# A first stage in written order with filter products ahead in several banks, and a recurrence whose first head has places of its own

## The chip, the cores and the metric

The kernel runs on one core of one Trainium2 chip. The metric is the time of one execution in device microseconds (us); lower is better. A core has a matrix engine (TensorE, PE), a vector engine (VectorE, DVE), a scalar engine for functions and copies (ScalarE, ACT), a general engine (GpSimd, POOL) and a queue that issues transfers (SyncE, SP). Each has its own in-order stream of instructions; they wait for each other by semaphores.

## The reference

Three blocks follow each other on one sequence of 512 positions with 1024 features. Only the first block and one part of the second matter here.

Block 1 norms x, scales and shifts it by a condition c, and gives the result h to three branches:

```
mod   = silu(c) @ w_ada + b_ada            # shift, scale, gate: 1024 values each
h     = rmsnorm(x) * norm_g * (1 + scale) + shift
a     = attention over 8 heads of 64 (q, k, v, z from h @ w_in; a table of relative positions as bias)
b     = gated linear recurrence over 8 heads of 128: f = lb + (1 - lb) * sigmoid(fb),
        state = f * state + (1 - f) * k v, output silu(qb) * state, gated by silu(zb)
x     = x + gate * ((sigmoid(ga) * (a @ w_a) + sigmoid(gb) * (b @ w_b)) @ w_out)
```

Block 2 holds a long convolution whose filter depends on the weights alone: a small network of three sine layers gives 512 filter values for each of 512 channels, times a decay; the convolution is done by its spectrum. It also holds an embedding p @ w_ple that is needed late. Neither depends on x, so the kernel computes both before everything else.

## The kernel before

Everything is kept transposed: eight tiles of 128 features by 512 positions. A matrix is multiplied in two parts, high and low, to keep fp32 accuracy: each weight (128 x 1024, a "raw" tile by DMA) is cast on ACT into `wh` (L110), and DVE or POOL subtracts to give `wl` (L111); each activation is split the same way (`split`, L202 and L204). `acc_T` (L128) then issues three matmuls for each 128 rows, so a projection (`proj_T`, L138) is 24 matmuls of 512 columns. There are four raw places, three places for split weights, and eight PSUM banks: three "mm", two "s", two "t", one "o".

A scheduler orders the instructions of each engine by its own simulated timeline, except inside `manual_schedule`, which keeps the written order for the engines named. Where a region's instructions fall among those written outside of it stays the scheduler's choice.

The first stage is `start` (L486). It loads and computes, side by side:

- the filter network: `layer` (L1198, three times: two small matmuls, seven DVE operations to reduce the angle, a sine on ACT), then `filt(t)` for four tiles of positions (two fp32 matmuls from 64 rows in the "s" banks, a product with the decay on DVE L1234, a sum and a difference L1241, and their splits), then `spectrum(f)` for two halves of the spectrum: per half 24 matmuls in the "mm" banks (function `halves`), copies by ACT (L1251, L1252), a sum and a difference on POOL, four stores issued by ACT (L1256);
- the embedding: `emb`, eight tiles of six matmuls, copied into tiles of A and stored;
- the condition's scale and shift: `AdaRows` (L453). Each loads eight rows of 128 x 1024 (tile `adar`, six places for both), and four matmuls of 32 x 256 for each row add up in the bank "o"; `columns` copies the sum out (`adarow`, L473) and turns it;
- the norm of x: squares on ACT (L513), added on DVE (L515), `col_sums`, `rsqrt` (a power on POOL, L251), `rows`;
- h: `x` is scaled on DVE (L525), then each of eight tiles gets its shift and is split into A (ACT L533, DVE L534);
- `rel_table`: a small table for the attention's bias, stored to memory.

Then `attn1` (L544) runs four pairs of heads. Before its last values it opens a region in which PE keeps the written order, which lasts through the recurrence `hgrn` (L755). `last_values` turns the softmax weights of the last pair by PE and multiplies them with v, four steps; between them it issues the 24 matmuls of the recurrence's first forget projection (`w1fb[0]`) as filler. `hgrn` opens a pool `hg` whose places overlap those of attention. `Head.f` makes tanh, Ln (L795, L796) and a scan over positions (L800) with `reset`; `gated` makes q and z (tanh on ACT, a DVE product); `between` and `operands` make for each of seven levels a difference of cumulated logarithms (POOL L841, L842), its exponential (ACT L843) and two products (DVE L846, L847); `products` multiplies them on PE.

## Time and profile before

| what | us |
|---|---|
| median of 3 runs (lowest, highest) | 2259.17 (2255.76, 2261.93) |
| the profiled execution's own time | 2263.86 |
| its span | 2262.1 |
| first projection of attention starts | 84.75 |
| first head's products on PE start | 256.79 |

The page shows one execution by the hardware profiler. Engine rows give busy time; rows of operations give the line, the engine, output<-inputs by tile names, shape and count; in square brackets stands the idle time before an operation and what released it. "PE" counts matmuls, "PEld" the loading of their weights. The clock is the share of full speed that TensorE was granted.

### The profile page before, as it was taken

How to read it: one execution, taken by the hardware profiler on the slowest of the kernel's cores; microseconds unless marked ns; L12 is line 12 of the kernel's file. 1: busy time of each engine (PE TensorE's matmuls, PEld its weight loads, DVE VectorE, ACT ScalarE, POOL GpSimd, SP SyncE). 2: the span in 40 equal slices, each digit the busy share in tenths (PEclk: the TensorE clock that was granted, in tenths of full speed). 3: DMA queues.
4: the chain of work that ended last, by engine and by line, in shares of the span. 5: the costliest groups of instructions: out<-in, count | busy, mean ns of one | idle time of the engine just before them, and what ended most of it. 6: DMA issues, size and time to landing. Idle time of an engine off the chain costs nothing.

```text
span 2262.1 us, 30194 instructions
## 1 busy us (share of the span) xinstructions
PE 2193.2 (97%) x11672; PEld 1793.4 (79%) x11672; DVE 1372.2 (61%) x2226; ACT 947.0 (42%) x1597; POOL 529.1 (23%) x454
## 2 busy tenths in 40 slices
PE   7898999999999998999999999999999999999998
PEld 4677788888888976688888886798888788888886
DVE  6564777753354598478647647877666754433333
ACT  4344556642243456544324434455544233222221
POOL 3233555521122225221001103000111221310220
PEclk7899999999999999999999999999999999999999
DMA  8552122224323342233232243222222422223322
GB/s 317 183 162 75 54 94 85 84 75 130 103 88 110 115 136 75 68 109 101 79 110 102 70 153 118 87 83 75 80 95 83 140 84 94 94 83 112 98 79 76
DMA packets 80728, 235.27 MB, mean 104 GB/s; under 512 B 9887, under 2 KB 10911, under 8 KB 80584
## 3 DMA queue, kind: packets, MB, share of 16 engines
q1 hardware_dynamic: 65768, 208.25, 28.2%
q10 hardware_dynamic: 14816, 25.08, 3.4%
q8 instruction: 92, 1.51, 0.3%
q14 instruction: 52, 0.43, 0.1%
HBM read 218.60 MB, written 15.22 MB: 103 GB/s over the span
## 4 chain that ended last, share of the span: by engine, by line
PE 56%; DVE 2%; issue 2%; ACT 1%; POOL 0%; POOLq 0%; DVEq 0%; ACTq 0%
PE mm L116 49%; PE s L116 3%; PE o L116 2%; PE t L116 1%; DVE sg L1772 0%; PE t L1612 0%; ACT wh L110 0%; DVE x L2438 0%; DVE st L1597 0%; DVE wl L111 0%; DVE x L1773 0%; DVE B L212 0%; PE t L2123 0%; ACT A L211 0%; PE t L2086 0%
## 5 line engine op out<-in xcount | busy, mean ns | idle before, releaser
L116 PE MATMUL mm<-A,wh 128*128 128x512 f32 x2176 | 691.1, 393 | 1.0 <-DVE A L212 1.0
L110 ACT CAST wh<-wr 128x1024 fp32r<-128x1024 f32 (+2 forms) x374 | 368.4, 987 | 609.6 <-PE mm L116 398.5
L111 DVE TENSOR_TENSOR wl<-wr,wh 128x1024 fp32r<-128x1024 f32 (+3 forms) x371 | 446.2, 1204 | 275.4 <-ACT wh L110 274.3
L116 PE MATMUL mm<-B,wh 128*128 128x512 f32 x1672 | 536.2, 396 | 1.3 <-DVE us L268 0.9
L116 PEld LDWEIGHTS mm<-A,wh 128*128 128x128 f32 x2176 | 409.6, 189 | 89.3 <-issue 1.9
L116 PE MATMUL mm<-A,wl 128*128 128x512 f32 x1088 | 425.8, 392 | 4.3 <-DVE wl L111 4.3
L116 PEld LDWEIGHTS mm<-B,wh 128*128 128x128 f32 x1672 | 313.5, 188 | 72.7 <-issue 4.0
L116 PE MATMUL mm<-B,wl 128*128 128x512 f32 x836 | 329.2, 394 | 0.0
L116 PEld LDWEIGHTS mm<-A,wl 128*128 128x128 f32 x1088 | 205.4, 189 | 47.7 <-DVE wl L111 6.3
L116 PEld LDWEIGHTS mm<-B,wl 128*128 128x128 f32 x836 | 157.3, 188 | 35.0 <-issue 3.0
L251 POOL TENSOR_TENSOR r<-r,mhalf 128x4 f32<-128x4 f32 (+1 forms) x40 | 53.2, 1332 | 407.6 <-DVE r L250 407.6
L116 PE MATMUL mm<-a,wh 128*128 128x512 f32 x448 | 140.5, 389 | 0.0
L268 DVE TENSOR_TENSOR us<-mm,bc 128x512 f32<-128x512 f32 x95 | 65.1, 688 | 97.2 <-PE mm L116 95.8
L204 POOL TENSOR_TENSOR a<-sl,a 128x512 fp32r<-128x512 f32 x28 | 40.5, 1446 | 274.2 <-ACT a L202 274.2
L116 PEld LDWEIGHTS mm<-a,wh 128*128 128x128 f32 x448 | 84.1, 188 | 17.5
L116 PE MATMUL mm<-a,wl 128*128 128x512 f32 x224 | 86.8, 389 | 0.0
L116 PE MATMUL mm<-wh,A 128*128 128x256 f32 x448 | 84.8, 285 | 0.0
L116 PEld LDWEIGHTS mm<-wh,A 128*128 128x128 f32 x448 | 71.0, 191 | 1.2 <-issue 0.6
L2358 POOL TENSOR_TENSOR sl<-sl,bc 128x512 f32<-128x512 f32 x22 | 28.7, 1305 | 167.6 <-DVE sl L1718 167.6
L116 PE MATMUL mm<-wl,A 128*128 128x256 f32 x224 | 63.6, 284 | 0.0
L116 PE MATMUL mm<-wh,B 128*128 128x256 f32 x320 | 61.2, 287 | 0.0
L1747 DVE TENSOR_TENSOR x<-x,mm 128x512 f32<-128x512 f32 x32 | 22.0, 687 | 64.5 <-PE mm L116 64.5
(588 smaller groups left out, 3472.0 us busy)
## 6 DMA issues: line engine op xcount, KB each, us to landing
wr<-w2upg SPq DMA_DIRECT2D x22, 512.0 KB, 3.4
wr<-w2upu SPq DMA_DIRECT2D x22, 512.0 KB, 3.4
wr<-w3fg SPq DMA_DIRECT2D x22, 512.0 KB, 3.4
wr<-w3fu SPq DMA_DIRECT2D x22, 512.0 KB, 3.4
adar<-w1ada SPq DMA_DIRECT2D x16, 512.0 KB, 7.6
wr<-w3out SPq DMA_DIRECT2D x16, 512.0 KB, 3.5
wr<-w1ib SPq DMA_DIRECT2D x14, 512.0 KB, 3.5
wr<-w2uh SPq DMA_DIRECT2D x12, 512.0 KB, 3.4
```

Of the source, the lines that this page charges most:

```text
L110: nc.scalar.copy(out=hi[:, :n], in_=r[:, :n])
L111: (eng or nc.vector).tensor_tensor(out=lo[:, :n], in0=r[:, :n], in1=hi[:, :n].bitcast(F32), op=ALU.subtract)
L116: return self.nc.tensor.matmul(out, a, b, start=start, stop=stop)
L204: eng.tensor_tensor(out=l[:p], in0=src, in1=hi[:p].bitcast(F32), op=ALU.subtract)
L251: nc.gpsimd.tensor_tensor(out=r, in0=r, in1=self.mhalf[:, :n], op=ALU.pow)
L268: self.nc.vector.tensor_tensor(out=out, in0=ps, in1=bc, op=ALU.mult)
L1747: k.nc.vector.tensor_tensor(out=xs[n], in0=xs[n], in1=ps, op=ALU.add)
L2358: nc.gpsimd.tensor_tensor(out=s, in0=s, in1=norm.bc, op=ALU.mult)
```

## The change

The first stage is written as one order for PE, ACT, DVE, POOL and SP. Modulation rows are stepped through two or four at a time instead of all at once; the scale rows have four places, the shift rows are loaded as halves into the tiles of A. Filter products are separated from their use (`filt_ps`, in "s" and "mm" banks by turns). All four sums and differences of the filters are on DVE, all their low parts on POOL. Embeddings and the copies of the spectrum get tiles `e0` to `e7` of their own; their stores are issued by SP, at the end of what they belong to. The first weight of attention (`w1q[0]`) is loaded and split inside the region and handed on in `k.first`.

In attention's end, the forget projection `w1fb[0]` is issued on PE ahead of `last_values`, whose filler is now `w1qb[0]`. The first head's `k`, `b` and `q` (h0), `lvl` and `reset` are in the outer pool, and the first tanh depends on the last exponential of the softmax. For the first head, the differences of levels 0 and 2 are on DVE. The four zero fills (`ADs`, `near`) come after the first operands.

The core of the diff:

```diff
 def proj_T(...)
-            self.acc_T(ps, self.w(s, nk * P, eng), act, nk, i == 0, i == len(nks) - 1, k0=k0)
+            w, self.first = self.first or self.w(s, nk * P, eng), None
+            self.acc_T(ps, w, act, nk, i == 0, i == len(nks) - 1, k0=k0)
...
 class AdaRows
-    def load(self):
+    def load(self, kks, places=None):
         k = self.k
-        for kk in range(NK):
-            self.r.append(self.pool.tile([P, D], F32, tag="adar", bufs=6, name=k.name("adar")))
-            k.nc.sync.dma_start(out=self.r[kk], in_=k.aps["w1ada"][self.part, kk])
+        for kk in kks:
+            src = k.aps["w1ada"][self.part, kk]
+            if places:
+                r = places[kk]
+                for j in range(2):
+                    k.nc.sync.dma_start(out=r[j], in_=src[:, j * T : (j + 1) * T])
+            else:
+                t = self.pool.tile([P, D], F32, tag="adar", bufs=4, name=k.name("adar"))
+                k.nc.sync.dma_start(out=t, in_=src)
+                r = (t[:, :T], t[:, T:])
+            self.r.append(r)
...
 def start(k, early):
-    with k.tc.tile_pool(name="b1s", bufs=1) as pool:
+    with k.tc.tile_pool(name="b1s", bufs=1) as pool, k.tc.manual_schedule(
+        engines={E.PE, E.Activation, E.DVE, E.Pool, E.SP}
+    ):
+        scale, shift = AdaRows(k, pool, 1), AdaRows(k, pool, 0)
         early.load0(pool)
+        rb, oh = rel_load(k, pool)
...
+        scale.load(range(4))
         early.load1()
...
+        places = [[t.bitcast(F32) for t in k.A(i)] for i in range(NK)]
+        shift.load(range(4), places)
...
+        early.layer(0)
+        early.parts(0)
+        early.sin()
+        early.parts(1)
+        early.emb(2)
+        early.layer(1)
+        early.emb(2)
+        early.sin()
+        early.layer(2)
+        square(2)
+        scale.step(2)
+        early.emb(2)
+        square(2)
+        early.sin()
+        scale.step(2)
+        scale.load(range(4, 8))
+        shift.load(range(4, 6), places)
+        early.load_fw(0)
+        shift.load(range(6, 8), places)
+        early.load_fw(1)
+        early.emb(2)
+        early.filt_ps(0)
+        square(4)
+        early.filt_ps(1)
+        sums = k.col_sums(acc)
+        early.filt(0)
+        r = k.rsqrt(sums, NT, 1.0 / D)
+        early.filt_ps(2)
+        shift.step(2)
+        bc = k.rows(r)
+        early.filt(1)
+        scale.step(4)
+        early.filt_ps(3)
+        early.store()
+        early.filt(2)
+        shift.step(2)
         sc1 = scale.columns()
+        early.fparts(0)
+        early.filt(3)
...
+        early.halves(0, 0)
+        shift.step(4)
         sh = shift.columns()
+        early.fparts(1)
+        tab = rel_table(k, rb, oh)
...
+            if i == 4:
+                early.halves(0, 1)
+
+        k.first = k.w(k.aps["w1q"][0])
+        early.halves(1, 0)
+        early.halves(1, 1)
+        early.sums()
...
 def last_values(pr, pts, v, z2):
-            w = k.w(k.aps["w1fb"][0])
+            w = k.w(k.aps["w1qb"][0])
...
                 ordered.enter_context(k.tc.manual_schedule(engines={mybir.EngineType.PE}))
+                ahead.append(k.proj_T([k.aps["w1fb"][0]], h))
                 ahead.append(last_values(pr, pts, cur[2], z2))
...
 class Head, f
+                tile = lambda tag, i: p.tile([P, T], F32, tag=tag, bufs=2, name=k.name(tag)) if hd else h0[i]
+                kk, b = self.kk, self.b = tile("k", 0), tile("b", 1)
+                t = nc.scalar.activation(out=kk, in_=ps, func=AF.Tanh, scale=0.5)
+                if hd == 0:
...
+                    k.tc.add_manual_dep(t.ins, k.last_exp.ins.name, info, reason="functions of the scalar engine")
...
 operands
+                    eng = nc.vector if self.hd == 0 and li in (0, 2) else nc.gpsimd
+                    eng.tensor_tensor(out=dv[:, :, 0], in0=mid, in1=bv[:, :, 0], op=ALU.subtract)
+                    eng.tensor_tensor(out=dv[:, :, 1], in0=bv[:, :, 1], in1=mid, op=ALU.subtract)
...
 hgrn, the loop over heads
             cur.operands(range(4))
+            if hd == 0:
+                for t in ADs + near:
+                    nc.gpsimd.memset(t, 0.0)
...
 block1
+        h0 = [op.tile([P, T], F32, tag=f"h0{i}", name=f"h0{i}") for i in range(3)]
+        lvl = op.tile([P, 256], F32, tag="lvl", name="lvl")
+        k.nc.scalar.dma_start(out=lvl, in_=k.aps["c_lvl"])
+        reset = op.tile([P, T], F32, tag="reset", name="reset")
+        k.nc.scalar.dma_start(out=reset, in_=k.aps["c_reset"])
...
 class Early2
+    def filt_ps(self, t):
+        k = self.k
+        r = slice(t // 2 * 64, t // 2 * 64 + 64)
+        self.fps[t] = []
+        for j in range(2):
+            ps = k.bank(*(("mm", 3) if t % 2 else ("s", 2)))
+            k.mm(ps, self.cur[r, t % 2 * P : t % 2 * P + P], self.wo[r, j * 512 : (j + 1) * 512], True, True)
+            self.fps[t].append(ps)
...
     def filt(self, t):
-            (nc.gpsimd if add else nc.vector).tensor_tensor(out=s, in0=fb[0], in1=fb[1], op=op)
-            l.append(k.split(k.pair(p, f"{nm}{t}"), s, lo="v" if add else "g"))
+            nc.vector.tensor_tensor(out=s, in0=fb[0], in1=fb[1], op=op)
+            l.append(k.split(k.pair(p, f"{nm}{t}"), s, lo="g"))
...
+    def fparts(self, f):
+        self.fw_parts.append(self.k.parts(self.cw[f], eng=None if f else self.k.nc.gpsimd))
...
+    def sums(self):
+        nc = self.k.nc
+        for f, j, (a, b) in self.ab:
+            d = self.tmp()
             nc.gpsimd.tensor_tensor(out=d, in0=a, in1=b, op=ALU.subtract)
-            nc.gpsimd.tensor_tensor(out=a, in0=a, in1=b, op=ALU.add)
+            nc.vector.tensor_tensor(out=a, in0=a, in1=b, op=ALU.add)
             for i, s in enumerate((a, d)):
-                nc.scalar.dma_start(out=self.kf[j, 2 * f + i], in_=s)
+                nc.sync.dma_start(out=self.kf[j, 2 * f + i], in_=s)
```

More of the change, by code (lines that the diff above doesn't have):

```diff
@@ L136, in acc_T @@
             self.mm(ps, wh, al[:, :n], False, stop and k == nk - 1)
+    first = None
     def proj_T(self, srcs, act, tag="mm", bufs=3, nks=(8,), eng=None):
@@ L495, in start @@
             xs.append(x)
+        scale.load(range(4))
         early.load1()
-        early.load_fw(0)
-        early.load_fw(1)
-        scale, shift = AdaRows(k, pool, 1), AdaRows(k, pool, 0)
-        scale.load()
+        places = [[t.bitcast(F32) for t in k.A(i)] for i in range(NK)]
+        shift.load(range(4), places)
         c = k.v("c", 0, 8)
@@ L537, in start @@
             h.append((hi, lo))
-        with k.tc.issue_after(mark):
-            early.spectrum(1)
-            tab = rel_table(k, pool)
+            if i == 4:
[4 more added lines that the diff above has]
+        early.sums()
     return h, tab
@@ L803, in qz @@
                 if i == 0:
-                    self.q = gated(self.hd, "w1qb", "q")
+                    first = {} if self.hd else {"ps": ps0[1], "o": h0[2]}
+                    self.q = gated(self.hd, "w1qb", "q", **first)
                 else:
@@ L961, in hgrn @@
         cur, old = Head(0), None
-        cur.f(f0)
+        cur.f(ps0[0])
         cur.qz(0)
@@ L1045, in block1 @@
             with ordered:
-                hgrn(k, h, *lb, ob, op, fill, v0, ahead[1])
+                hgrn(k, h, *lb, ob, op, fill, (v0, ahead[1:], h0, lvl, reset))
             return block1_end(k, h, oa, ob, gate, first, xp(), done)
@@ L1179, in load0, with parts @@
         self.fw = [self.load(nm, 64) for nm in ("fw1", "fw2", "fw3")]
-        self.cw, self.sm, self.df = [], [], []
-        pt = [p.tile([P, T], F32, tag=f"pt{i}", name=f"pt{i}") for i in range(2)]
+        self.cw, self.sm, self.df, self.we, self.pa, self.es = [], [], [], [], [], []
+        self.ws, self.fw_parts, self.ab = [], [], []
+        self.pt = [p.tile([P, T], F32, tag=f"pt{i}", name=f"pt{i}") for i in range(2)]
         for i in range(2):
-            nc.sync.dma_start(out=pt[i], in_=k.aps["pT"][:, i * T : (i + 1) * T])
-        self.we = [k.parts(k.raw(k.aps["w2ple"][i]), eng=None) for i in range(2)]
-        self.pa = [k.split(k.pair(p, f"pa{i}"), pt[i], lo="g") for i in range(2)]
+            nc.sync.dma_start(out=self.pt[i], in_=k.aps["pT"][:, i * T : (i + 1) * T])
+            self.ws.append(k.raw(k.aps["w2ple"][i]))
+    def parts(self, i):
+        k = self.k
+        for j in (0, 1) if i == 0 else ():
+            self.pa.append(k.split(k.pair(self.p, f"pa{j}"), self.pt[j], lo="g"))
+        self.we.append(k.parts(self.ws[i]))
     def load1(self):
@@ L1211, in layer, with sin, emb @@
         clamp_pi(k, h)
-        nc.scalar.activation(out=h, in_=h, func=AF.Sin)
         self.cur = h
-    def emb(self, ns):
+    def sin(self):
+        self.k.nc.scalar.activation(out=self.cur, in_=self.cur, func=AF.Sin)
+    def emb(self, m):
         k, p, nc = self.k, self.p, self.k.nc
-        for n in ns:
+        for n in range(len(self.es), len(self.es) + m):
             hi, lo = self.we[n // 4]
@@ L1221, in emb, with store @@
             k.acc_T(ps, (hi[:, o:], lo[:, o:]), self.pa, 2)
-            e = k.A(n)[0].bitcast(F32)
+            e = p.tile([P, T], F32, tag=f"e{n}", name=f"e{n}")
             nc.scalar.copy(out=e, in_=ps)
-            nc.sync.dma_start(out=self.ed[n], in_=e)
+            self.es.append(e)
+    def store(self):
+        for n, e in enumerate(self.es):
+            self.k.nc.sync.dma_start(out=self.ed[n], in_=e)
+    def filt_ps(self, t):
+        k = self.k
+        r = slice(t // 2 * 64, t // 2 * 64 + 64)
[4 more added lines that the diff above has]
+            self.fps[t].append(ps)
+    fps = {}
     def filt(self, t):
@@ L1228, in filt @@
         fb = []
-        for j in range(2):
-            ps = k.bank("s", 2)
-            r = slice(t // 2 * 64, t // 2 * 64 + 64)
-            k.mm(ps, self.cur[r, t % 2 * P : t % 2 * P + P], self.wo[r, j * 512 : (j + 1) * 512], True, True)
+        for ps in self.fps[t]:
             f = self.tmp()
```

90 lines of the change are left out of this document (43 added, 47 removed).

## The prediction

> **What bounds the kernel now.** I read the page first: is one engine the bound, and where is it not full?
>
> ```profile
> span 2262.1 us, 30194 instructions
> ...
> PE 2193.2 (97%) x11672; PEld 1793.4 (79%) x11672; DVE 1372.2 (61%) x2226; ACT 947.0 (42%) x1597; POOL 529.1 (23%) x454
> ...
> GB/s 317 183 162 75 54 94 85 84 75 130 103 88 110 115 136 75 68 109 101 79 110 102 70 153 118 87 83 75 80 95 83 140 84 94 94 83 112 98 79 76
> ```
>
> TensorE (PE) is busy for 97% of the span, and after its first slice DMA moves half or a third of what it moved there. So almost any microsecond by which the stream of projections starts earlier, or by which a hole in it closes, comes off the end. Next the waits of PE over the whole span, and stretches of it:
>
> ```profile
> PE t L647 <- POOL p L632: 6.1, 6, 2.4
> ...
> PE s L116 <- DVE qk L847: 4.4, 1, 4.4
> PE mm L116 <- DVE wl L111: 4.3, 6, 0.8
> ...
> PE o L116 <- DMA adar<-w1ada: 4.2, 2, 4.1
> ```
>
> ```profile
> 0.00:84.75 84.75, 63.78 (x276) 34.11 (x277) 50.02 (x74) 34.19 (x56) 28.53 (x28) 0.78 0.69 257
> 216.50:224.10 7.60, 1.69 (x5) 0.73 (x6) 4.30 (x14) 3.42 (x11) 6.21 (x5) 0.75 0.44 138
> ...
> 235.40:256.80 21.40, 17.03 (x81) 13.84 (x77) 16.72 (x20) 11.98 (x17) 14.81 (x19) 0.94 0.26 90
> ```
>
> Columns of the second view: stretch, length, busy time of PE, weight loads, DVE, ACT, POOL, granted clock, DMA share, GB/s. PE's idle time in the whole span is 2262.1 - 2193.2 = 69 us, and nearly half lies in the two places that the change rewrites: the first stage (until the first projection starts at 84.75 us; PE idle for 84.75 - 63.78 = 21 us, mean clock 0.78), and the passage from attention to the recurrence (7.60 - 1.69 = 5.9 us idle at 216.5 to 224.1, where PE waits for POOL's softmax scaling, and 4.4 us before 256.8 for the first head's operands).
>
> **The change, first stage.** I cut it into three legs at fixed events.
>
> ```profile
> 31.81 0.69 DVE L1234 TENSOR_TENSOR tmp<-s,dec 128x512 f32<-128x512 f32 x1 [1.66 <-PE s L116]
> ...
> 55.83 1.36 DVE L204 TENSOR_TENSOR sm<-tmp,sm 128x512 fp32r<-128x512 f32 x1 [1.21 <-ACT sm L202]
> ```
> ```profile
> 74.79 0.37 ACT L473 COPY adarow<-o 128x256 f32<-128x256 f32 x1 [11.56 <-PE o L116]
> 76.14 5.02 ACT L533 ACTIVATE A<-x,adac 128x512 fp32r<-128x512 f32 x8 [0.98 <-DVE adac L478]
> ```
> ```profile
> 30.65 1.98 PE L116 MATMUL s<-fwo,fh 64*128 64x512 f32 x4 [1.80 <-ACT fh L1212]
> 32.56 1.94 PE L116 MATMUL o<-adar,silc 128*32 128x256 f32 x16
> ...
> 40.01 2.07 PE L116 MATMUL s<-fwo,fh 64*128 64x512 f32 x2
> ...
> 53.34 1.05 PE L116 MATMUL mm<-df,wh 128*128 128x512 f32 x2
> ...
> 54.62 0.63 PE L116 MATMUL mm<-df,wh 128*128 128x512 f32 x1
> ...
> 58.10 1.07 PE L116 MATMUL o<-adar,silc 128*32 128x256 f32 x16
> ...
> 82.08 1.24 PE L116 MATMUL t<-oh,rb 33*8 33x512 f32 x4
> ...
> 84.75 0.39 PE L116 MATMUL mm<-A,wh 128*128 128x512 f32 x1
> ...
> 85.22 0.62 PE L116 MATMUL mm<-A,wh 128*128 128x512 f32 x2
> ```
>
> Before, the filters begin at 31.8 us, their last split ends at 55.83 + 1.36 = 57.2 (leg 1, 25.4 us), the shift row is copied out at 75.2 (leg 2, 18.0 us), and the first projection starts at 84.75 (leg 3, 9.6 us).
>
> Start of the filters: the written order puts all eight embeddings, squares and additions ahead of them on PE, ACT and DVE. Before, the scheduler had the same work done by about then. I take 32.4 (+0.6), between 31 and 34.
>
> Leg 1, the filters:
>
> ```profile
> L1241 DVE TENSOR_TENSOR tmp<-tmp,tmp 128x512 f32<-128x512 f32 x4 | 6.0, 1493 | 0.6 <-POOL tmp L1237 0.6
> ...
> L1234 DVE TENSOR_TENSOR tmp<-s,dec 128x512 f32<-128x512 f32 x8 | 5.5, 690 | 9.5 <-PE s L116 8.5 <-issue 1.0
> ```
> ```profile
> L1241 POOL TENSOR_TENSOR tmp<-tmp,tmp 128x512 f32<-128x512 f32 x4 | 7.0, 1762 | 6.8 <-DVE tmp L1234 6.7
> L204 POOL TENSOR_TENSOR df<-tmp,df 128x512 fp32r<-128x512 f32 x4 | 5.1, 1274 | 3.8 <-ACT df L202 3.8
> ...
> L111 POOL TENSOR_TENSOR wl<-wr,wh 128x1024 fp32r<-128x1024 f32 x1 | 2.7, 2667 | 0.5 <-ACT wh L110 0.5
> L251 POOL TENSOR_TENSOR r<-r,mhalf 128x4 f32<-128x4 f32 x1 | 1.0, 1022 | 14.2 <-DVE r L250 14.2
> ```
>
> DVE waited 8.5 us for filter products, since two "s" banks hold one step only; four banks ("s" and "mm" in turn) let PE run a step ahead, so that wait goes. The four sums (7.0 us) leave POOL for DVE, and all eight low parts go to POOL. DVE then has per step two products (0.69 each) and two sums (0.69 free, 1.49 beside POOL): 2.8 to 4.4, four steps 11 to 17.4 us. POOL has 8 x 1.27 low parts, 2.67 for one spectrum weight and 1.02 for the norm's power: 13.9 us, beginning some 3.5 us after DVE (five operations of about 0.7 stand before the first low part): 17.4 us at least, with no slack. PE has four products left (two steps ran ahead) at 2.07 = 8.3, eight rows of modulation weights at 1.94 for two = 7.8, and the norm's rows, some 2: 18 us. What is late next is thus POOL, with PE close. The written order puts the 2.67 in front of the last step's low parts, so I take 20.5; ends 17.4 and 25.4 (no gain). Gain 4.9.
>
> Leg 2: before, PE waited here for the modulation rows (the 4.2 us for adar above). The last loads could only be issued when products had freed their places:
>
> ```profile
> 58.80 0.34 SPq L463 DMA_DIRECT2D adar<-w1ada x1
> ...
> 61.80 4.42 SPq L463 DMA_DIRECT2D adar<-w1ada x3
> ```
>
> Now the shift rows land in the tiles of h, which are empty until then: 16 issues of 256 KB. On SP they stand behind each other: the first four rows wait for nothing, the last four behind four scale rows that wait for the second step on PE (about 26 us). All loads up to the last spectrum weight are about 15.3 MB (16 modulation rows of 512 KB, x with 2 MB, the rest constants); even at the 317 GB/s of the first slice they are in by 48 us, and the shift rows are wanted after 50. The embeddings' stores (2 MB) move behind them. So this wait is hidden. Left in leg 2 are 12 spectrum products and the last four shift rows. Two in a row took 1.05 us slow and 0.62 fast, one alone 0.63 and 0.39, hence they follow each other by 0.42 or 0.23 us: 12 are 2.7 to 5.1. Four rows are 2 x 1.07 to 2 x 1.94; the copy 0.4. Sum 5.2 to 9.4; I take 7.4, the middle, since the rows and filters leave the clock low and the spectrum raises it. Gain 10.6.
>
> Which clock? Between 30.65 and 57.9 PE has no gap, yet a filter product went from 0.99 us (1.98 for two) to 2.07, and eight row products from 1.07 to 1.94: these matmuls use 64 of the rows or 32 of the columns. The Trainium skill ("TensorE: Matmul & The Clock Gate", Part 1) says that the gate opens after about 3.4 us of a busy PE and closes after as much idleness; by it the new, gapless order would run fast throughout. The row speaks against that for narrow matmuls, so my sum has them slow; the rule's result is the third rival.
>
> Leg 3: 24 spectrum products and the table's matmuls before; now 36, and w1q's weight is loaded and split in line, behind the table's store on SP and six casts on ACT. PE: 36 x 0.23 to 0.42 = 8.3 to 15.1, the table 1.2, two transposes 0.7: 10.2 to 17. ACT in its order: a weight cast (0.99, page row L110 below), the eight casts of h (5.02), four copies at 5.02 / 8 = 0.63, w1q's cast: 9.5. I take 12 (cold start, then fast): loss 2.4, ends +0.6 and +5.4 (some of 17 is shared with ACT). The spectrum's eight stores go from ACT's queue to SP's, where they may stand before the next weights: none to 5.5 us (one projection), I take 1.0, as the scheduler may still place loads between them.
>
> Sum of the stage: +0.6 - 4.9 - 10.6 + 2.4 + 1.0 = -11.5 us; ends about -20 and +1.
>
> **The change, passage to the recurrence.**
>
> ```profile
> 239.07 0.60 ACT L795 ACTIVATE k<-mm 128x512 f32<-128x512 f32 x1 [2.14 <-DVE hog L781]
> 239.69 1.28 ACT L796 ACT_TABLE_LOAD   x1
> 240.98 0.82 ACT L796 ACTIVATE b<-k,lb 128x512 f32<-128x512 f32 x1
> ```
> ```profile
> 242.41 1.33 DVE L800 TENSOR_TENSOR_SCAN b<-reset,b 128x512 f32<-128x512 f32 x1 [4.14 <-DMA reset<-c_reset]
> ```
> ```profile
> 256.79 3.20 PE L116 MATMUL s<-qk 128*64 128x64 f32 x56 [4.37 <-DVE qk L847]
> ```
> ```profile
> L847 DVE TENSOR_TENSOR qk<-d,q 128x256 f32<-128x256 f32 x4 | 4.1, 1030 | 0.0
> L846 DVE TENSOR_TENSOR qk<-d,k 128x256 f32<-128x256 f32 x5 | 3.8, 759 | 0.0
> ```
>
> Before, the first forget projection fills PE between the transposes, and tanh, logarithm and scan wait until attention's places come free (about 238 us) and reset has landed; the scan ends at 243.7, the operands take 13 us more. Now that projection (24 x 0.23 = 5.5 us) runs in the 5.9 us where PE waited for POOL, the next one (qb) takes its place as filler, and tanh, Ln and scan run from about 222 us in places of their own. Behind the waiting tanh on ACT stand only its own Ln and the copies of the turned weights, which come later anyway; had it come before an exponential, a table load of 1.28 would be paid twice. The operands still live where attention's tiles were, so they start when attention ends, some 1.1 us sooner by the warmer clock (the first six fillers ran slow, 6 x 0.19): about 236.9 instead of 243.8. But DVE takes two levels of differences to its products: one operation on 128x256 is (4.1 + 3.8) / 9 = 0.88 on average, so 4 x 0.88 beside 8 x 0.88; with Q and kd (384 columns, some 0.95 each), the q and z gates (0.69 each, as the filters' products) and a weight's low part (1.4, two of those) that is 15.2 us. The operands are ready at 252.1, against 256.7. PE is done with its other work at about 245 and waits longer than before. The gain is what the operands gain: 4.6 us; ends 0 and 8 (DVE not binding).
>
> **Sum.** -11.5 - 4.6 = -16.1 us against the profiled execution's own 2263.86 us (span 2262.1): 2247.8. That run lies 4.7 above the median of the runs, 2259.17, which gives **2243**.
>
> **Rivals.** First, in-order queues: the filters stay at 25.4 us and leg 3 takes 15, because ACT, DVE and SP now block on what is written next. +0.6 + 0 - 10.6 + 5.4 + 1.0 - 4.6 = -8.2: 2251. For it: ACT's copies now stand behind the cast of w1q. Chance 0.20. Second, the passage gains nothing, as the operands wait for attention's places and DVE has 3.5 us more: -11.5, 2248; chance 0.13. Third, PE keeps its clock: legs 2 and 3 at 5.2 and 10.2: +0.6 - 4.9 - 12.8 + 0.6 + 1.0 - 4.6 = -20.1, 2239; chance 0.12. Fourth, slower: only PE is ordered by hand after the stage, and the scheduler lays the other engines' work anew. In the rest of the kernel
>
> ```profile
> L110 ACT CAST wh<-wr 128x1024 fp32r<-128x1024 f32 (+2 forms) x374 | 368.4, 987 | 609.6 <-PE mm L116 398.5
> ```
>
> 374 weights are split, and PE waited for six, 0.7 us each (4.3 us above). From 24 more such waits on, the 16.1 us are gone; 30 more cost 21 and give 2264. Against it: three weight places, filled a projection ahead. Chance 0.05.
>
> **How the numbers follow.** The forecast has 0.48, other mixtures 0.02. About 0.3%, 6.8 us, is what a measurement of this kernel can tell from no change. From the cases: faster 0.87 (the forecast, the third rival, nearly all of the first two), same 0.08, slower 0.05. The range reaches from both best ends (-28, 2231) to the first rival with a little more lost (-6, 2253).
>
> **What would show it.** Right: the first projection at 70 to 75 us; the last shift row without a wait for DMA; DVE's wait for filter products gone; the scan before 230 us and the first head's products near 251 us, with PE's wait there above 4.4 us. Wrong: the first projection after 80 us, a new wait of PE for w1k's weight, filter products at 0.99 throughout, or a later start of some stage behind 300 us that gives the gain back.

## The result, and the profile after

| what | us |
|---|---|
| before, median of 4 runs (lowest, highest) | 2257.47 (2255.35, 2261.93) |
| after, median of 4 runs (lowest, highest) | 2245.42 (2244.72, 2246.51) |
| ratio after to before (95% interval) | 0.9945 (0.9928 to 0.9962) |
| the profiled execution of after: its time, its span | 2245.16, 2243.3 |

The kernel after is about 0.5% faster, 12.05 us by the medians; the forecast was 2243.0 and a gain of 16.1. The first projection starts at 74.06 us (84.75 in the profile before), the first head's products start at 241.12 (256.79). One execution of a later kernel (`full_rows`) took 2934.05 us at a granted clock of 0.69 over its whole span; it is left out of that kernel's numbers.

The page of after, span and busy times, first:

```profile
span 2243.3 us, 30191 instructions
...
PE 2179.1 (97%) x11672; PEld 1787.8 (80%) x11672; DVE 1374.5 (61%) x2234; ACT 948.8 (42%) x1597; POOL 519.8 (23%) x446
```

PE has as many matmuls as before. Its busy time is 14 us below that of the first profile of before (2193.2), but a second profile of before (an experiment below) has the same 2179.1: that difference lies between executions of one program and is not the change. Next the waits of PE over the span (total, times, longest):

```profile
...
PE t L116 <- POOL r L254: 4.6, 2, 3.2
...
PE t L718 <- POOL p L703: 4.0, 2, 3.8
PE t L116 <- DVE adac L500: 3.0, 1, 3.0
PE s L116 <- DVE qk L923: 2.9, 1, 2.9
```

The wait for the modulation rows (adar, 4.2 us) is gone. Two new ones stand in its place: for the norm's power on POOL (3.2 us at one place) and for the scale's and shift's columns on DVE (adac, 3.0). PE's timeline shows where (start, duration, in brackets the idle time before and what ended it):

```profile
35.34 1.98 PE L116 MATMUL s<-fwo,fh 64*128 64x512 f32 x4
37.25 1.56 PE L116 MATMUL mm<-A,silc 128*32 128x256 f32 x16
42.01 2.08 PE L116 MATMUL t<-ident,r 128*128 128x128 f32 x8 [3.20 <-POOL r L254]
44.02 3.64 PE L116 MATMUL o<-adar,silc 128*32 128x256 f32 x32
47.59 2.13 PE L116 MATMUL mm<-fwo,fh 64*128 64x512 f32 x4
...
62.69 0.59 PE L116 MATMUL t<-oh,rb 33*8 33x128 f32 x2 [3.04 <-DVE adac L500]
...
74.06 0.40 PE L116 MATMUL mm<-A,wh 128*128 128x512 f32 x1
```

And POOL's and DVE's, where these two waits come from:

```profile
38.78 1.75 POOL L207 TENSOR_TENSOR df<-tmp,df 128x512 fp32r<-128x512 f32 x1
40.48 1.47 POOL L254 TENSOR_TENSOR r<-r,mhalf 128x4 f32<-128x4 f32 x1
...
55.30 1.73 POOL L207 TENSOR_TENSOR df<-tmp,df 128x512 fp32r<-128x512 f32 x1
```
```profile
51.13 0.17 DVE L500 TENSOR_TENSOR adac<-t,vec 128x8 f32<-128x8 f32 x1 [7.53 <-PE t L498]
...
54.02 8.54 DVE L588 SCALAR_TENSOR_TENSOR x<-x,gada,bc 128x512 f32<-128x512 f32 x8
62.47 0.16 DVE L500 TENSOR_TENSOR adac<-t,vec 128x8 f32<-128x8 f32 x1
```

The chain through the stage reads like this. The power, one operation on 128x4, stands on POOL behind the first filter step's two low parts and ends at 41.95. PE waits for it before it can turn r, and so the scale rows and the last filter products (47.59) come late. On DVE the scale's columns (51.13) are written ahead of the last filter step, so DVE idles 7.53 us for them; for most of that time the last step's own products, which begin at 47.59, were not there either. The scaling of x then takes 8.54 us, the shift's columns stand behind it (62.47), and the casts into h behind these. In the legs of the prediction, with the second profile of the kernel before (an experiment below) beside them:

| leg, us | before, first profile | before, second profile | forecast | after |
|---|---|---|---|---|
| start of the filters | 31.8 | 32.35 | 32.4 | 34.2 |
| filters, to the last low part | 25.4 | 20.2 | 20.5 | 22.8 |
| to the shift row's copy | 18.0 | 16.8 | 7.4 | 1.2 |
| to the first projection | 9.6 | 8.2 | 12 + 1 | 15.9 |
| first projection | 84.75 | 77.61 | 73.3 | 74.06 |

### The profile page after: what moved, and what is told of

It is laid out like the page before. It is cut to its first block, busy times and chain, and to the rows that moved or that the text cites. A ratio compares the mean times of both kernels' runs of the same rounds, so it can differ in the third digit from the quotient of the medians.

```text
span 2243.3 us, 30191 instructions
## 1 busy us (share of the span) xinstructions
PE 2179.1 (97%) x11672; PEld 1787.8 (80%) x11672; DVE 1374.5 (61%) x2234; ACT 948.8 (42%) x1597; POOL 519.8 (23%) x446
## 4 chain that ended last, share of the span: by engine, by line
PE 57%; DVE 2%; issue 2%; ACT 1%; POOL 0%; POOLq 0%; DVEq 0%; ACTq 0%
PE mm L116 50%; PE s L116 3%; PE o L116 2%; PE t L116 1%; DVE sg L1888 0%; PE t L1728 0%; ACT wh L110 0%; DVE x L2554 0%; DVE st L1713 0%; DVE wl L111 0%; DVE x L1889 0%; DVE B L215 0%; PE t L2239 0%; ACT A L214 0%; PE t L2202 0%
## 5 line engine op out<-in xcount | busy, mean ns | idle before, releaser
L207 POOL TENSOR_TENSOR a<-sl,a 128x512 fp32r<-128x512 f32 x28 | 40.5, 1447 | 273.9 <-ACT a L205 273.9
```

Source lines behind the costliest of these rows:

```text
L207: eng.tensor_tensor(out=l[:p], in0=src, in1=hi[:p].bitcast(F32), op=ALU.subtract)
```

## The experiments

Two numbers of each single profile are used most: when the first projection starts, and how long after it the first head's products start. The rest of the span behind the products lasted between 1997 and 2007 us in these profiles, in kernels that change nothing there, so a single total tells no more than some 5 us (10 at the widest).

Both numbers vary too. Four kernels have the first stage of after unchanged (after, stage_only, places, levels_pool): their first projections start at 74.06, 73.72, 73.29 and 74.46, within 1.2 us, so 2 us or more between single profiles of this stage are taken as a difference. The distance from there to the products lies between 167.06 and 169.33 in seven kernels whose passage is the same (after, shared4, passage_only, power_early, two_banks, sums_pool, late_table). In the two short ones, after and shared4, PE's last wait for POOL's softmax scaling ends 141.0 and 141.3 us behind the first projection, and the clock was 0.83 in the ten microseconds from 140 us on; in the five others that wait ends at 141.6 to 142.4, and the clock was 0.66. Here are these ten microseconds of after and passage_only (columns as in the prediction):

```profile
214.06:224.06 10.00, 9.02 (x37) 5.90 (x37) 2.79 (x4) 2.68 (x4) 2.66 (x2) 0.83 0.10 39
```
```profile
218.47:228.47 10.00, 7.56 (x28) 5.42 (x28) 2.81 (x5) 3.70 (x6) 3.29 (x2) 0.66 0.18 52
```

So some 2 us of that distance vary with attention's last stretch, where the change was the same. Why is not shown.

### Each half of the change alone

`stage_only` is the kernel before with the whole of `start` and `Early2` as changed, and attention's end and the recurrence as before. `passage_only` is the opposite.

```diff
-    with k.tc.tile_pool(name="b1s", bufs=1) as pool:
+    with k.tc.tile_pool(name="b1s", bufs=1) as pool, k.tc.manual_schedule(
+        engines={E.PE, E.Activation, E.DVE, E.Pool, E.SP}
+    ):
```

The first line of each: this one is in `stage_only` alone, the next in `passage_only` alone.

```diff
+        h0 = [op.tile([P, T], F32, tag=f"h0{i}", name=f"h0{i}") for i in range(3)]
```

> The first stage of the changed kernel, with attention's end and the recurrence as before. Theory (two gains that add up): the first projection at 74 us as in the changed kernel, the first head's products 172 us after it as before, PE's 4.4 us wait for them back; time 10 to 11 us under the kernel before. Rival (the passage's gain is lost again later, and the 12 us are the stage alone): the time is 12 us under it.

> Attention's end and the recurrence of the changed kernel, with the first stage as before. Theory: first projection at 84.7 us, the first head's products 167 us after it (172 before); time 4 to 5 us under the kernel before. Rival (lost again later): within 1.5 us of the kernel before.

| kernel | median, us | ratio to before (95%) | first projection | products behind it |
|---|---|---|---|---|
| stage_only | 2247.72 (5 runs) | 0.9957 (0.9941 to 0.9974) | 73.72 | 169.86 |
| passage_only | 2253.44 (10 runs) | 0.9978 (0.9965 to 0.9991) | 78.47 | 169.33 |
| before, in these runs | 2256.77 (14 runs) | 1 | | |

The stage is worth 9.05 us and the passage 3.33; their sum, 12.4, is near what the whole change gave (12.05), within intervals that reach some 3 or 4 us to either side. By the medians both rivals fall: no gain of the passage is lost again later. But several expected numbers missed. The gains fall short of 10 to 11 and of 4 to 5 us; in stage_only the products follow after 169.86 us and not 172, though PE's wait for them is back (4.36); in passage_only they follow after 169.33 and not 167. And passage_only has the stage of before, with PE's instructions in the same order, and its first projection came at 78.47, not at 84.75. That last one is the key to the rest.

### The kernel before once more

> The kernel before, unchanged, a second profile. The profiled execution that the prediction rests on took 2263.86 us with its first projection at 84.75 us; the run with the passage alone changed has the same order on PE in the first stage and began it at 78.47. Theory: the stage before has no fixed length, since the stretch at a clock of 0.50 falls differently in each execution, and the predicted run was a slow one: first projection between 76 and 82 us, and fewer 2-us windows at 0.50 between 32 and 57 us than the twelve of the first profile. Rival: the written edits outside of the stage moved it, and the stage before is 84.75 us long each time: first projection within 1 us of 84.75. In both, the first head's products follow 172 us (plus or minus 1.5) after the first projection.

2254.17 us, first projection at 77.61, products 250.50 - 77.61 = 172.9 behind it (172.0 in the first profile). The first row is the stretch from 32 to 57 us in the profile that the prediction used, the second the same stretch of the second profile (columns as in the prediction: busy PE, weight loads, DVE, ACT, POOL, granted clock, DMA share, GB/s):

```profile
32.00:57.00 25.00, 25.00 (x66) 10.35 (x65) 15.38 (x17) 6.21 (x10) 12.62 (x9) 0.52 0.70 275
```
```profile
32.00:57.00 25.00, 18.54 (x87) 7.32 (x85) 18.73 (x18) 8.73 (x14) 15.82 (x11) 1.00 0.75 296
```

In one execution PE had the clock at 0.52 and got through 66 matmuls, in the other at 1.00 and through 87. The program is the same. PE's rows of the second, to be read beside those in the prediction (30.65 to 49.47):

```profile
31.19 1.98 PE L116 MATMUL s<-fwo,fh 64*128 64x512 f32 x4 [1.80 <-ACT fh L1212]
33.10 1.07 PE L116 MATMUL o<-adar,silc 128*32 128x256 f32 x16
34.10 1.98 PE L116 MATMUL s<-fwo,fh 64*128 64x512 f32 x4
...
40.46 1.12 PE L116 MATMUL s<-fwo,fh 64*128 64x512 f32 x2 [0.18 <-DVE tmp L1234]
```

Same wait of 1.80 us, same order; the 16 row products take 1.07 us here and 1.94 there. Three profiles of this stage now stand at 84.75, 77.61 and 78.47. So the forecast's base was the slow end of a stage that varied by 7 us between executions, and it counted the difference as the change's gain.

### Does the width of the filter products hold the clock low?

```diff
-        nc.scalar.activation(out=h, in_=h, func=AF.Sin)
+        if i == 2:
+            self.cz = [p.tile([P, 256], F32, tag=f"cz{a}", name=f"cz{a}") for a in range(2)]
+            for a, z in enumerate(self.cz):
+                nc.gpsimd.memset(z, 0.0)
+                r = slice(a * 64, a * 64 + 64)
+                nc.scalar.activation(out=z[r], in_=h[r], func=AF.Sin)
+        else:
+            nc.scalar.activation(out=h, in_=h, func=AF.Sin)
...
-            r = slice(t // 2 * 64, t // 2 * 64 + 64)
-            k.mm(ps, self.cur[r, t % 2 * P : t % 2 * P + P], self.wo[r, j * 512 : (j + 1) * 512], True, True)
+            k.mm(ps, self.cz[t // 2][:, t % 2 * P : t % 2 * P + P], self.wo[:, j * 512 : (j + 1) * 512], True, True)
```

The kernel before with filter products that read all 128 rows; 64 of them hold zeros.

> The kernel before, with the filter products from all 128 rows (half of them zeros in the left operand) instead of 64; the output is the same. Theory (the clock is held low between 32.5 and 56 us because the products use 64 rows): granted clock back at 1.0 by 40 us, a filter product at about 1 us from there, first projection 1 to 4 us earlier. Rival (it is held low by pauses of PE of a microsecond or two that recur, whatever the rows): clock 0.5 until 55 us or so, a product at 2.07, first projection within 1 us of 84.75.

> The kernel before, its filter products reading all 128 rows (the other 64 hold zeros) instead of 64. The prediction's step: matmuls of 64 rows hold the clock low; by it the median is 3 us or more below that of the kernel before, and the clock is at full speed while the filters run in the profile. Rival: the rows do not matter, and the low stretch falls where it falls: median within 2 us of before's, times as widely spread as its own (some 12 us), and the clock may be low or high while the filters run.

The first profile's execution took 2256.43 us; its clock fell at 32 us as in the first profile of before, was back after 3.4 us (before: 24 us) and was low once more from about 46 to 49 us; the first projection came at 78.17. The second profile had the clock at full speed while the filters ran, as the second of before with its 64 rows. The median of nine executions is 2255.49 beside 2256.1 (ratio 0.9997, 0.9987 to 1.0007): the width is worth nothing on average, and the prediction's step that narrow matmuls run slow falls as a rule. One part of the rival missed as well: the nine executions lie within 4 us (2253.93 to 2257.89), while before spread over 9 us in the same batch. Of the 38 executions of before beside these experiments 14 were above 2258 us, and none of these nine. That the full rows shorten a low stretch once it has begun, and cost a little otherwise, would fit; it isn't shown.

### The power on POOL

```diff
-        early.filt(0)
-        r = k.rsqrt(sums, NT, 1.0 / D)
+        rs = []
+        early.filt(0, lambda: rs.append(k.rsqrt(sums, NT, 1.0 / D)))
+        r = rs[0]
...
-    def filt(self, t):
+    def filt(self, t, mid=None):
...
+        if mid:
+            mid()
         for op, l, nm in ((ALU.add, self.sm, "sm"), (ALU.subtract, self.df, "df")):
```

The kernel after, with the power issued between the first filter's products with the decay and its sums and low parts.

> The changed kernel, with the norm's power on POOL ahead of the first filter step's two low parts instead of behind them. Theory (PE's 3.2 us wait for this power starts a chain: slow clock, fourth filter step late, x scaled late, h late): no wait of PE for the power, the last filter low part at 52 instead of 57.0, the scaling of x over at 56 to 57 instead of 62.6, the first projection at 68 to 69; time 5 us under the changed kernel. Rival (POOL's 14 us of low parts and the weight set the end of the filters): the first projection within 1.5 us of 74.

2239.34 us (4 runs, 2238.27 to 2243.63), ratio 0.9922 (0.9902 to 0.9943); the first projection at 70.57. The rival falls. The theory has the direction, but promised more of the stage: the last low part ends at 54.53 (52 expected), the scaling of x at 60.09 (56 to 57), and the first projection was to come at 68 to 69. This is the fastest kernel of the study. Its POOL, then its PE, where the wait of 3.20 us is gone:

```profile
35.98 1.01 POOL L254 TENSOR_TENSOR r<-r,mhalf 128x4 f32<-128x4 f32 x1
37.47 1.28 POOL L207 TENSOR_TENSOR sm<-tmp,sm 128x512 fp32r<-128x512 f32 x1 [0.47 <-ACT sm L205]
```
```profile
37.22 1.93 PE L116 MATMUL mm<-A,silc 128*32 128x256 f32 x16
39.09 1.83 PE L116 MATMUL t<-ident,r 128*128 128x128 f32 x8
```

A single operation of 1 us, moved ahead of two others of its engine, took 3.5 us off the stage, about as much as the whole rewritten stage gained on the second profile of before (77.61 - 74.06). Between the medians lie 6.1 us (2245.42 and 2239.34, from two batches); where the rest comes from isn't shown.

The first link of the theory's chain is not as it said: PE's wait doesn't start the slow clock. In after the wait begins at 38.81, and the granted clock had already fallen to 0.50 before 38 us; in power_early, without the wait, it fell between 37 and 38 us as well. What differs is its return: at about 47.9 us in after, at about 40.5 in power_early.

### Banks, sums, places of the shift

`two_banks` gives the filter products the two "s" banks alone; `sums_pool` puts the filters' sums back on POOL and their low parts back on DVE; `shared4` loads shift rows 4 to 7 into the scale's places, once these are free, instead of into the tiles of h. Their edits against after, in this order:

```diff
-            ps = k.bank(*(("mm", 3) if t % 2 else ("s", 2)))
+            ps = k.bank("s", 2)
```
```diff
-            nc.vector.tensor_tensor(out=s, in0=fb[0], in1=fb[1], op=op)
-            l.append(k.split(k.pair(p, f"{nm}{t}"), s, lo="g"))
+            (nc.gpsimd if add else nc.vector).tensor_tensor(out=s, in0=fb[0], in1=fb[1], op=op)
+            l.append(k.split(k.pair(p, f"{nm}{t}"), s, lo="v" if add else "g"))
```
```diff
-        shift.load(range(4, 6), places)
...
-        shift.load(range(6, 8), places)
...
         early.filt_ps(3)
+        shift.load(range(4, 8))
```

> The kernel after, its filter products in the two s banks alone, as before, the rest unchanged. The prediction's step: four banks are what ends DVE's wait for filter products, so with two it comes back (4 us or more in all), the last low part ends after 60 us and the first projection starts at 77 us or later. Rival: the chain through the norm's power on POOL and PE's wait for it set the filters' end, the banks do not: last low part within 1 us of 57.0, first projection within 1.5 us of 74.06, PE's wait for r still 4 us or more in all.

> The kernel after, the filters' four sums on POOL and the low part of each sum on DVE again, as before. Prediction's step: POOL is the engine that is late in the filters, so four operations of 1.7 us there for four of 1.3 to 1.7 less leave it where it was; last low part within 1.5 us of 57.0 and first projection within 1.5 us of 74.06. Rival (DVE's and POOL's chain with hops between them costs more): last low part after 59 us, first projection after 76 us.

> The kernel after, its shift rows 4 to 7 loaded into the scale's four places once the scale's products have freed them (about 46 us) instead of into the tiles of h. The prediction's step: places of their own are what hides the shift's loads, so without them PE waits for adar before the last four rows and the first projection starts 4 us or more later (78 us or more). Rival: since the scaling of x on DVE ends at 62.6 us and the shift is not wanted earlier, rows that land by about 57 us cost nothing: first projection within 1.5 us of 74.06.

| kernel | last low part ends | first projection | time of one execution |
|---|---|---|---|
| after | 57.03 | 74.06 | 2245.16 |
| two_banks | 59.57 + 1.72 = 61.29 | 76.23 | 2246.95 |
| sums_pool | 60.00 + 1.28 = 61.28 | 77.35 | 2251.44 |
| shared4 | 54.49 + 1.73 = 56.22 | 72.98 | 2243.84 |

Two banks: the filters end 4.3 us later, as the prediction's step has it, and the first projection 2.2 us later, between the two expectations. Both views had something, and neither is whole. It is not DVE that waits for filter products again (1.0 us, where 4 were expected); PE now waits for DVE to empty a bank. POOL's power costs PE nothing in this stage any more (the 1.4 us below lie elsewhere and are there in before too). The clock was at 0.50 from 33 to 49 us here, so part of the 4.3 us may be the clock's.

```profile
PE s L116 <- DVE tmp L1340: 3.9, 2, 3.0
...
PE t L116 <- POOL r L254: 1.4, 1, 1.4
```

Sums on POOL: the first expectation falls and the rival holds. The first counted operations per engine, and POOL is in fact busy for less time there (its operations from the first zero fill to the last low part add up to 14.0 us, 15.5 in after); but each half of a step now runs through three engines. The last step, DVE first, then POOL:

```profile
53.89 0.68 DVE L1340 TENSOR_TENSOR tmp<-mm,dec 128x512 f32<-128x512 f32 x1
57.98 0.69 DVE L207 TENSOR_TENSOR sm<-tmp,sm 128x512 fp32r<-128x512 f32 x1 [3.41 <-ACT sm L205]
58.59 0.68 DVE L1347 TENSOR_TENSOR tmp<-tmp,tmp 128x512 f32<-128x512 f32 x1
```
```profile
53.71 2.35 POOL L111 TENSOR_TENSOR wl<-wr,wh 128x1024 fp32r<-128x1024 f32 x1
56.02 1.28 POOL L1347 TENSOR_TENSOR tmp<-tmp,tmp 128x512 f32<-128x512 f32 x1
60.00 1.28 POOL L207 TENSOR_TENSOR df<-tmp,df 128x512 fp32r<-128x512 f32 x1 [2.71 <-ACT df L205]
```

The sum waits on POOL for the weight's low part, DVE's low part waits for the sum and its cast, the difference stands behind it on DVE, and POOL waits for the difference's cast. So moving the sums to DVE is worth 3.3 us of the stage, by these rows through its shorter chain and not through POOL's load.

Shared places: the prediction's step falls for the four rows that this kernel moves. They are issued at 44.53, into places that the scale used before, and are on time; the stage is no longer for it.

```profile
44.53 2.71 SPq L477 DMA_DIRECT2D adar<-w1ada  x4
```

For these rows, what ended the wait of the kernel before is that the loads are issued some 14 us earlier (its last ones went out at 58.80 and after), not the places of their own. Rows 0 to 3 still had such places, so no run shows the stage without any.

### The passage: places of the first head, levels on DVE

```diff
-                tile = lambda tag, i: p.tile([P, T], F32, tag=tag, bufs=2, name=k.name(tag)) if hd else h0[i]
+                tile = lambda tag, i: p.tile([P, T], F32, tag=tag, bufs=2, name=k.name(tag))
...
-                    first = {} if self.hd else {"ps": ps0[1], "o": h0[2]}
+                    first = {} if self.hd else {"ps": ps0[1]}
```

> The kernel after, the first head's k, b and q in the places of the recurrence's pool again (they lie where attention's tiles were); the projections ahead, lvl and reset stay as changed. After, the scan is at 215.93 us and the first head's products are 167.06 us behind the first projection. Theory (what passage gained comes from tanh, Ln and scan being done while attention ends): without places they wait for attention's end again, the scan moves behind 228 us, and the products follow 170 us or more after the first projection. Rival (the prediction's step: the operands wait for attention's end in any case and DVE's 15.2 us set the products, the early scan being hidden): scan late, products still 166 to 168.5 us after the first projection.

```diff
-                    eng = nc.vector if self.hd == 0 and li in (0, 2) else nc.gpsimd
+                    eng = nc.gpsimd
```

> The kernel after, the first head's differences of levels 0 and 2 on POOL again, as for the other levels. Theory (POOL is not what the operands wait for): products 165.5 to 168.5 us after the first projection, PE's wait for qk between 1.5 and 4.5 us. Rival (POOL sets the operands, four differences more on it cost 3 us): products 169.5 us or more after the first projection.

| kernel | scan | products | behind the first projection | PE's wait for qk |
|---|---|---|---|---|
| before, two profiles | 242.41, 235.93 | 256.79, 250.50 | 172.0, 172.9 | 4.4, 4.4 |
| after | 215.93 | 241.12 | 167.1 | 2.9 |
| places | 234.03 | 248.90 | 248.90 - 73.29 = 175.6 | 4.9 |
| levels_pool | 216.12 | 243.90 | 243.90 - 74.46 = 169.4 | 5.5 |

Without places of their own the scan is late and the products come 8.5 us later, even later than in the kernel before. Some 2 of these belong to attention's last stretch, which had the clock at 0.66 here too. Counted from attention's end, which DVE's L850 marks, the products follow after 18.2 us here (248.90 - 230.72) and after 11.8 in after (241.12 - 229.32), so the places are worth 6.4 us. The profile shows why the rival fails: the early scan isn't hidden, since scan, logarithm and table load come back onto the chain between attention's end (about 230.6) and the first level's differences. DVE of this kernel:

```profile
230.72 0.15 DVE L850 TENSOR_SCALAR hog<-vec 128x1 f32<-128x1 f32 x1
231.89 0.69 DVE L846 SCALAR_TENSOR_TENSOR q<-th,mm 128x512 f32<-128x512 f32 x1 [1.02 <-ACT th L843]
234.03 1.22 DVE L873 TENSOR_TENSOR_SCAN b<-reset,b 128x512 f32<-128x512 f32 x1 [1.44 <-ACT b L869]
235.28 0.82 DVE L917 TENSOR_TENSOR d<-b 128x256 f32<-128x256 f32 x1
```

And DVE of after at the same place, with the scan done 12 us earlier:

```profile
215.93 1.23 DVE L873 TENSOR_TENSOR_SCAN h<-reset,h 128x512 f32<-128x512 f32 x1 [2.60 <-ACT h L869]
...
228.53 0.69 DVE L207 TENSOR_TENSOR oa<-of,oa 128x512 fp32r<-128x512 f32 x1
229.32 0.15 DVE L850 TENSOR_SCALAR hog<-vec 128x1 f32<-128x1 f32 x1
229.40 0.42 DVE L917 TENSOR_TENSOR d<-h 128x256 f32<-128x256 f32 x1
229.73 1.05 DVE L918 TENSOR_TENSOR d<-h 128x256 f32<-128x256 f32 x1
```

The levels on POOL give a wait of 5.5 us where after and every other kernel with the changed passage have 2.9 to 3.0, outside of what "POOL is not what the operands wait for" allowed, and products 2.4 us later, just short of the rival's 169.5. Attention's last stretch was like that of after (clock 0.83), and from attention's end the products follow after 14.4 us (11.8): the two levels on DVE are worth about 2.5 us there. The whole execution took 2245.37 us, as long as after; one execution can't say whether those 2.5 us reach the end.

### A candidate that lost

The edit against power_early:

```diff
         bc = k.rows(r)
+        early.fparts(0)
         early.filt(1)
...
-        early.fparts(0)
         early.filt(3)
...
+        early.halves(0, 1)
         early.fparts(1)
-        tab = rel_table(k, rb, oh)
...
             if i == 4:
-                early.halves(0, 1)
+                tab = rel_table(k, rb, oh)
```

> A candidate. The kernel power_early (the norm's power on POOL ahead of the first filter's low parts; 2239.34 us, first projection 70.57) with two moves more: the first spectrum weight's low part on POOL ahead of the second filter's low parts (PE waited 1.88 us for it), and the second part of the first spectrum (12 matmuls) ahead of the table of positions, whose wait for DVE behind the scaling of x was 1.74 us. Theory: the stage still loses to instructions that stand behind others in written order, so both waits go and the first projection starts at 66 to 69.5 us, the time is 2235 to 2239. Rival: the scaling of x on DVE and the casts of h then set the first projection, which stays within 1 us of 70.57, and the time within 2 us of 2239.3. In both the kernel beats before and after.

2248.98 us (6 runs), ratio 0.9965 (0.9951 to 0.9978): faster than before, slower than after and power_early; the first projection at 75.69. Both expectations miss. The two waits did go (the spectrum's second part ran from 56.96 on, 60.52 in power_early), but another came:

```profile
PE mm L116 <- ACT ab L1363: 4.3, 1, 4.3
```
```profile
61.43 5.01 ACT L600 ACTIVATE A<-x,adac 128x512 fp32r<-128x512 f32 x8
71.38 1.04 ACT L110 CAST wh<-wr 128x1024 fp32r<-128x1024 f32 x1 [4.94 <-DMA wr<-w1q]
72.33 1.55 ACT L1363 COPY ab<-mm 128x512 f32<-128x512 f32 x3
```
```profile
67.27 0.28 SPq L414 DMA_DIRECT2D scr_tab<-oh  x1
67.61 0.33 SPq L97 DMA_DIRECT2D wr<-w1q  x1
```

Read from the bottom up: on SP the load of w1q stands behind the store of the table, and the table was moved behind half of h. So the weight goes out at 67.61 (62.57 in power_early); ACT's cast of it waits 4.94 us; the spectrum's copies stand behind the cast; PE waits 4.3 us for the banks that they empty. In both kernels the load goes out 0.34 us after that store. By these rows the loss isn't the table's matmuls but the store that it issues. The two moves were made together, and no run has one of them alone.

## Why the prediction was right, and where its sum was not

The time, 2245.42, lies in the range, and the direction and most mechanisms hold. The gain was 12.05 us, not 16.1. Step by step:

- **The base.** "I cut it into three legs at fixed events", of one execution. This is the step that failed. That execution ran its filters at a clock of 0.52, another of the same kernel at 1.00, and their first projections differ by 7.1 us. The correction to the median of the runs, 4.7 us, was subtracted from the total but not from the stage, where the excess lay; taken from the stage it gives a gain of 11.4. Against the second profile the stage gained 3.6 us at the first projection; stage_only puts the whole worth of the rewritten stage at 9.05 us, with what follows it.
- **The stage's sum**, forecast -11.5, measured -10.7 against the first profile (84.75 to 74.06). That this is near is luck: the misses of the four legs below (+1.8, +2.3, -6.2 and +2.9 us) cancel. Its ends were too narrow as well: those of its terms add up to about -21 and +4.5, not -20 and +1.
- **Start of the filters**, forecast +0.6, measured +2.4 (34.22; 32.35 in before's second profile): just past the range that was given for it (31 to 34).
- **Filters**, forecast -4.9, measured -2.6 against the first profile, and +2.6 against the second (22.8 after 20.2). DVE's wait for filter products is gone, as forecast, and with two banks the filters end 4.3 us later. "What is late next is thus POOL, with PE close" holds in the sense of a chain, not of a load: POOL's busy time was not the limit, its order was, with the power behind two low parts. That row, 1.02 us, was in the sum of POOL's load; that PE waits for it was not.
- **Shift row**, forecast -10.6, measured -16.8: the wait for adar went as said, and the leg overlaps the filters' end, since the first spectrum part needs only the sums. The cause was mis-stated: for the last rows it is the earlier issue, not the places (shared4).
- **To the first projection**, forecast +2.4 and 1.0 for the stores, measured +6.3, within its end (+5.4 and 1.0). The forecast listed PE's and ACT's work and left out DVE's: the scaling of x, moved beside POOL's low parts, 8.54 us instead of 5.39, with the shift's columns behind it.
- **Passage**, forecast -4.6, measured between -3.3 (passage_only, by medians) and -5.0 (products behind the first projection, 172.04 to 167.06). Two terms were off and cancelled, which is luck again. The projection "runs in the 5.9 us where PE waited for POOL": PE had done it (24 matmuls from 201.9 to 209.0) before its longest wait for POOL's scaling began at 211.3, and it still waits 4.0 us there, after 6.1 (5.8 in the second profile), so some 2 of the 5.5 us were hidden. So attention's end came 229.2 - 74.1 = 155.1 us behind the first projection, 1.8 us later than before (238.0 - 84.75 = 153.3) and not 1.1 sooner. In return the operands took 11.9 us from there and not 15.2, since the first level's differences begin at once and many DVE operations on 128x256 took 0.41 us, not 0.88. (With two low parts the terms listed for the 15.2 add up to 16.6; the sum counts one.) So the sign "with PE's wait there above 4.4 us" was wrong: 2.9.
- **The clock.** That narrow matmuls run slow holds not as a rule (full_rows, passage_only, and before's second profile with 64 rows at 1.00). One sign of being wrong did appear, "filter products at 0.99 throughout": three of the four steps in after ran at 0.94 to 0.99 us for a product, as the row at 35.34 does, and the last at 1.07. The low stretch, 38 to 48 us, lay between the third and the fourth.
- **A sign with the wrong number.** The sign "the first head's products near 251 us" leaves out the stage's own 11.5 us; with them the forecast's sum is 240.6, and 241.12 was measured.

Of the rivals, the first (in-order queues) has the right mechanism at another place: not ACT behind w1q's cast in the filters, but POOL's power and DVE's columns; late_table then shows it at w1q's cast. Its last leg, 15 us and 1.0 for the stores, is what came (15.9); its filters, 25.4 us, are not (22.8), and power_early takes 3.5 us more off the stage. The second (the passage gains nothing) falls by passage_only. The third (PE keeps its clock, legs 2 and 3 at 5.2 and 10.2): the two legs took 17.0 us together, with the clock at 0.80 from 58 to 64 us and 0.63 from 64 to 70, so the shorter legs did not come about. The fourth, some 30 more waits for weights, didn't come: seven waits for wl, six before.

## What to carry to other kernels

Before a stage is cut into legs, compare two executions of the same program: a leg that varies by 7 us must not be counted as the change's gain. When an order is written by hand, look for short instructions that another engine waits for and that stand behind long ones, and count a moved step's DMA issues as well: 1 us of POOL moved forward gave 3.5 us of stage, and a table moved back took 5 with the load behind its store. Loads are hidden by early issue; places of their own are only one way to it. And two profiles are best compared from the event nearest to the change: from attention's end to the products after and passage_only agree on 11.8 us, while from the first projection they differ by 2.3.

## What the runs showed of the hardware that was not expected

The granted clock of one stage differs between executions with the same instructions on PE: 0.52, 1.00 and 0.86 between 32 and 57 us in before, before again and passage_only. The Trainium skill ("TensorE: Matmul & The Clock Gate", Part 1) says that the window which watches PE runs freely and that the count of cold matmuls differs from run to run; the trace agrees with the second, and no run here shows the window. It also gives about 3.4 us of busy PE until the gate opens, and here the trace differs: in the first profile PE shows 25.00 us busy of 25.00 at a mean clock of 0.52. Why it stayed low that long is open. The rewritten stage is steadier: in after, stage_only, places and levels_pool the clock fell to 0.50 between 36 and 39 us and came back between 46 and 49, each time.

DVE beside POOL: the eight scalings of x, 128x512 each, in after, first while POOL works, then while it rests (columns: stretch, length, busy time of these operations on DVE, clock, DMA share, GB/s):

```profile
54.00:58.70 4.70, 4.68 (x3) 1.00 0.01 3
58.70:62.60 3.90, 3.86 (x6) 0.87 0.00 0
```

Three began in 4.70 us beside POOL, about 1.6 us each, and the rest went at about 0.7; in the kernel before all eight took 5.39 us, with no POOL instruction beside them (the last of the five busy times; columns as in the prediction):

```profile
65.08:70.47 5.39, 3.16 (x40) 1.19 (x32) 5.39 (x8) 0.00 (x0) 0.00 (x0) 0.82 1.01 377
```

So DVE's scaling took longer where POOL's work was moved beside it; here up to 3.15 us of it stand on the chain to the first projection, since the shift's row was there at 58.19 and its columns came at 62.47.
